# A list scheduler's rules for tiles in advance, changed for the two stages of layer 1's mixer

## The chip, the cores and the metric

The kernel runs on one core of one Trainium2 chip. The metric is the device time of one execution in microseconds (us). Three runs of the kernel before gave a median of 2732.69 us (2731.06 to 2735.65).

## What is computed

A diffusion backbone of two layers over 1024 latent tokens and 256 context tokens, 1024 channels, all in 32-bit floats. Each layer is a mixer and a SwiGLU feed-forward network (FFN), both between RMS norms with learned modulation:

```
for l in range(DEPTH):
    h  = modulate(x, g_pre_mix[l], sh_m, sc_m)
    hc = modulate(ctx, g_pre_mix[l], csh_m, csc_m)
    if l % 2 == 0:
        y, yc = even_mixer(h, hc, ...)
    else:
        y, yc = odd_mixer(h, hc, ...)
    x = x + gt_m * rmsnorm(y, g_post_mix[l])
    h = modulate(x, g_pre_ffn[l], sh_f, sc_f)
    x = x + gt_f * rmsnorm(swiglu(h, w_ffn_in[l], w_ffn_out[l]), g_post_ffn[l])
    ...
return x
```

Layer 0's mixer is dense attention beside a pooling mixer. Layer 1's, the odd one, is attention of 16 heads (4 for keys and values) in a window of 128 tokens on each side plus all context tokens and a sink logit per head. The context stream (`ctx`) is updated in layer 0 only.

## The kernel before, in words

Activations lie transposed: 128 channels on the partitions, tokens along the free axis. The latent tokens are two chunks of 512, L0 and L1; the context is a chunk of 256, CC. Every matmul product is made of three, so that rounded operands give nearly 32-bit results: weights and activations are split in a rounded part (names ending in h: `wh`, `hh`, `th`) and the remainder (`wl`, `hl`, `tl`), and high times high, high times low and low times high are added in one PSUM bank. A weight unit of 128 rows (`wunit`) is loaded into a tile `raw` by a DMA that SP issues; ACT copies it, rounded, to `wh`; DVE (or, for some, POOL) subtracts to get `wl`. A norm is: ACT squares the tile (`S_sq`), DVE adds the squares, PE sums them over partitions with a matrix of ones, ACT takes the root and DVE the reciprocal (`rs`), PE spreads it over the partitions again (`S_rb` against `ident`), and DVE applies it.

`tile_dit` (from L429) doesn't issue instructions. It calls helpers that record operations in a plan, and `Plan.layout` (L241) then writes one order for each engine: it is a list scheduler that always places the operation that can start first by its own estimates of cost and latency. `emit` (L418) issues them in that order, so every profile row carries the line L421. Engines execute their own list in order and meet through semaphores.

Tiles come from three kinds of buffers, which the scheduler assigns too: 38 large ones of 128x1024 (tag Q: `raw`, `wh`, `wl`, `hh`, `yf` and so on), 19 small ones of 128x512 (tag S), and the 8 PSUM banks (tag p). `fits` (L283) refuses an operation that would open a new tile when no buffer is free, when the program in its recorded order would need all of them before that place, and in a third case that the change concerns: `AHEAD_OF` (L32) gives, for each of eight stages, a number `near` and for each kind a number of buffers kept back. An operation whose tile has its first place more than `near` operations past the first one that isn't placed yet may only take a buffer while more than the kept-back number are free.

The stage is the number in `plan.phase` when an operation is recorded. The stages around the change, in the order in which they are recorded:

- stage 7: layer 0's paired FFN, then `ffn_out` (L934) for L0 and CC. Its last group of four weight units gives the products ps_3502 to ps_3512 and ps_3529 to ps_3534 below; `chain` (L626) then applies the norm behind the FFN and the one ahead of the mixer for L0 and CC;
- stage 3: layer 1's projections for L0 and CC (`proj1`, L1462), and attention of L0's first half (`attend1`, L1484), between which `ffn_out` for L1 is spread as filling work (`merge`, L213);
- stage 4: projections for L1, attention of L0's second half and then of L1, with the gate products of the second FFN (`ffn_gates`, L758) as filling work; last `pair_up` (L976), which normalizes L1's result (`postnorm`, L616) and makes from it and L0's the five combinations `th`, `tl` (`prenorm_pair`, L589);
- stages 5 and 6: layer 1's paired FFN (`ffn_pair`, L780) and its output. For every unit `ffn_pair` adds and subtracts raw weights on DVE (`Q_sw`), rounds them on ACT and multiplies them with `th`, `tl`.

Of the kernel before, what the change touches and what calls it, by code (L numbers as in the profile page):

```python
# [28 lines left out]

NQ, NS = 38, 19  # L30
AHEADS = (90, 60, 100, 90, 80)
AHEAD_OF = ((100, {'p': 2, 'Q': 2, 'S': 2}), (250, {'p': 0, 'Q': 10, 'S': 2}), (150, {'p': 2, 'Q': 6, 'S': 0}), (100, {'p': 2, 'Q': 10, 'S': 6}), (250, {'p': 1, 'Q': 4, 'S': 0}), (250, {'p': 1, 'Q': 4, 'S': 2}), (250, {'p': 1, 'Q': 4, 'S': 0}), (250, {'p': 1, 'Q': 4, 'S': 2}))  # L32
MODLATE = (2, 3, 4)
POOLE = 4
OUTM = ("0", "c")
# [35 lines left out]
class Plan:  # L71
# [169 lines left out]
    def layout(self):  # L241
# [41 lines left out]
        def fits(i):  # L283

            for t in ops[i][5]:
                if t not in live:
# [3 lines left out]
                    if a > front and prof[tag][front:a].max() >= self.tag_bufs[tag]:  # L290
                        return tag
                    near, res = AHEAD_OF[ops[i][10]]
                    if a > front + near and len(slots[tag]) <= res.get(tag[0], 0):
# [1360 lines left out]
```

## Time and profile before

| what | value |
|---|---|
| median of three runs | 2732.69 us |
| profiled execution, its own time | 2732.75 us |
| its span in the trace | 2731.0 us |
| granted TensorE clock, mean | 0.982 |
| PE busy | 2617.1 us (96%) |
| DVE busy | 2072.2 us (76%) |
| ACT busy | 1389.4 us (51%) |
| POOL busy | 320.6 us (12%) |

The engines are PE (matrix products), DVE and ACT (elementwise), POOL (elementwise, slower) and SP, which here issues the DMAs. The busy shares are means over stages with different limits; what an order can change is read in the stretch where it changes. Times in the rows are microseconds from the start of the span; "[3.29 <-DVE Q_wl L421]" at the end of a row means that the engine sat idle for 3.29 us until DVE's instruction on Q_wl released it. A granted clock of 1.00 is TensorE's upper level, 2.4 GHz, 0.50 the lower, 1.2 GHz.

### The profile page before, as it was taken

The numbers are of one execution on the slowest core, as the hardware profiler recorded it, in microseconds if no ns is written. First come the engines' busy times: TensorE is split into PE (matmuls) and PEld (weight loads), VectorE is DVE, ScalarE is ACT, GpSimd is POOL, SyncE is SP. The second block draws the span as 40 slices with busy tenths as digits, with TensorE's granted clock in tenths as the row PEclk, the third lists the DMA queues.
The fourth block names the chain that finished last, engine by engine and source line by source line (L and its number), as shares of the span: only waits on it lengthen the run. The fifth ranks groups of instructions, "written<-read, shape, count | busy, mean of one in ns | idle before, by whom it ended". The sixth has DMA issues, their size and how long they took to land.

```text
span 2731.0 us, 39441 instructions
## 1 busy us (share of the span) xinstructions
PE 2617.1 (96%) x13685; PEld 2168.4 (79%) x13685; DVE 2072.2 (76%) x3816; ACT 1389.4 (51%) x2894; POOL 320.6 (12%) x277
## 2 busy tenths in 40 slices
PE   8989898999999999999999998998999999999997
PEld 4766677888888888888877888777878778887887
DVE  5779887866449999875485688898884699896655
ACT  4468875666544333331043467677775544444211
POOL 0354532000020000000011400220000300000001
PEclk9999999999999999999999998999999999999999
DMA  7334467333556666786533634435336547668662
GB/s 286 113 104 144 139 205 281 112 115 118 187 186 213 226 206 231 240 301 242 202 137 112 223 120 166 132 134 157 108 109 216 192 164 252 225 245 332 224 239 78
DMA packets 247176, 506.24 MB, mean 185 GB/s; under 512 B 25280, under 2 KB 86976, under 8 KB 246976
## 3 DMA queue, kind: packets, MB, share of 16 engines
q1 hardware_dynamic: 246976, 503.71, 53.4%
q8 instruction: 108, 1.77, 0.3%
q14 instruction: 92, 0.75, 0.1%
HBM read 363.11 MB, written 136.58 MB: 183 GB/s over the span
## 4 chain that ended last, share of the span: by engine, by line
PE 72%; DVE 10%; ACT 4%; issue 2%; DMA 2%; POOL 1%; SPq 0%; DVEq 0%; ACTq 0%; POOLq 0%
PE ps L421 72%; DVE Q_x L421 1%; DVE S_fw L421 1%; DVE ps L421 1%; DVE mx L421 1%; ACT S_ph L421 1%; ACT Q_p L421 1%; DVE Q_hl L421 1%; DVE Q_yf L421 1%; DVE S_sq L421 1%; DVE Q_tl L421 1%; DVE Q_wl L421 1%; ACT S_p L421 1%; DVE S_pl L421 1%; DVE S_t L421 1%
## 5 line engine op out<-in xcount | busy, mean ns | idle before, releaser
L421 PE MATMUL ps<-Q_ac,Q_wh 128*128 128x512 f32 (+1 forms) x1792 | 492.3, 356 | 0.8 <-ACT Q_wh L421 0.5
L421 PE MATMUL ps<-Q_hh,Q_wh 128*128 128x512 f32 (+1 forms) x992 | 364.6, 377 | 7.0 <-ACT Q_hh L421 3.5
L421 PE MATMUL ps<-Q_hl,Q_wh 128*128 128x512 f32 (+1 forms) x992 | 361.5, 373 | 1.9 <-DVE Q_hl L421 1.7
L421 PEld LDWEIGHTS ps<-Q_ac,Q_wh 128*128 128x128 f32 x1792 | 319.8, 191 | 45.5 <-DVE Q_yf L421 0.6
L421 PE MATMUL ps<-Q_ac,Q_wl 128*128 128x512 f32 (+1 forms) x896 | 317.5, 356 | 6.6 <-DVE Q_wl L421 6.6
L421 ACT ACTIVATE Q_wh<-Q_raw 128x1024 fp32r<-128x1024 f32 (+1 forms) x202 | 203.8, 1028 | 218.3 <-DMA Q_raw<-in_w_ffn_out 105.4
L421 DVE TENSOR_TENSOR Q_wl<-Q_raw,Q_wh 128x1024 fp32r<-128x1024 f32 (+1 forms) x190 | 226.6, 1202 | 95.8 <-ACT Q_wh L421 91.4
L421 PE MATMUL ps<-Q_tl,Q_wh 128*128 128x512 f32 x704 | 276.2, 392 | 2.6 <-DVE Q_tl L421 2.6
L421 PE MATMUL ps<-Q_th,Q_wh 128*128 128x512 f32 x704 | 275.9, 392 | 1.9 <-ACT Q_th L421 1.8
L421 PE MATMUL ps<-Q_kt,S_q 128*128 128x256 f32 (+3 forms) x992 | 254.4, 339 | 17.4 <-DVE Q_x L421 7.2
L421 DVE TENSOR_TENSOR S_pl<-ps,S_ph 128x512 fp32r<-128x512 f32 (+1 forms) x328 | 213.2, 671 | 70.5 <-ACT S_ph L421 65.7
L421 PE MATMUL ps<-Q_hh,Q_wl 128*128 128x512 f32 (+1 forms) x992 | 265.8, 372 | 0.0
L421 DVE TENSOR_TENSOR Q_yf<-Q_yf,ps 128x512 f32<-128x512 f32 (+1 forms) x220 | 130.1, 597 | 164.3 <-PE ps L421 163.8
L421 ACT ACTIVATE S_ph<-ps 128x512 fp32r<-128x512 f32 (+1 forms) x328 | 186.1, 604 | 88.6 <-PE ps L421 86.8
L421 PEld LDWEIGHTS ps<-Q_hh,Q_wh 128*128 128x128 f32 x992 | 189.6, 191 | 39.0 <-ACT Q_hh L421 5.1
L421 PEld LDWEIGHTS ps<-Q_hl,Q_wh 128*128 128x128 f32 x992 | 189.5, 191 | 30.3 <-DVE Q_hl L421 3.6
L421 PEld LDWEIGHTS ps<-Q_kt,S_q 128*128 128x128 f32 x992 | 170.6, 194 | 46.4 <-issue 11.4
L421 PEld LDWEIGHTS ps<-Q_hh,Q_wl 128*128 128x128 f32 x992 | 175.0, 190 | 27.4
L421 PE MATMUL ps<-ident,Q_p 128*128 128x128 f32 x928 | 185.7, 278 | 10.7 <-DVE S_pl L421 3.0
L421 PEld LDWEIGHTS ps<-Q_ac,Q_wl 128*128 128x128 f32 x896 | 171.0, 191 | 29.9 <-DVE Q_wl L421 7.9
L421 ACT ACTIVATE Q_p<-ps,nb 128x256 f32<-128x256 f32 (+1 forms) x336 | 185.5, 562 | 15.1 <-DVE nb L421 14.6
L421 PE MATMUL ps<-Q_th,Q_wl 128*128 128x512 f32 x704 | 188.8, 390 | 0.0
(198 smaller groups left out, 5379.8 us busy)
## 6 DMA issues: line engine op xcount, KB each, us to landing
Q_raw<-in_w_ffn_in SPq DMA_DIRECT2D x132, 512.0 KB, 4.6
mw<-in_w_mod SPq DMA_DIRECT2D x160, 256.0 KB, 3.6
Q_raw<-in_w_ffn_out SPq DMA_DIRECT2D x66, 512.0 KB, 6.3
a_scr_l<-S_act SPq DMA_DIRECT2D x112, 256.0 KB, 2.6
Q_ac<-a_scr_l SPq DMA_DIRECT2D x56, 512.0 KB, 5.9
t_scr<-S_act SPq DMA_DIRECT2D x112, 256.0 KB, 2.2
Q_ac<-t_scr SPq DMA_DIRECT2D x56, 512.0 KB, 5.7
S_q<-q_scr_l SPq DMA_DIRECT2D x192, 128.0 KB, 3.5
```

What stands on the lines that cost most here:

```text
L421: getattr(eng.real, op)(*args, **kw)
```

## The change

One line: two of the eight entries of `AHEAD_OF`, those of stages 3 and 4. Stage 3 may open tiles up to 300 operations ahead freely instead of 100, and past that keeps back 8 large and 3 small buffers instead of 10 and 6. Stage 4 does so for 150 operations instead of 250 and past that keeps back two small buffers where it kept none; its four large ones and the PSUM entries stay.

```diff
-AHEAD_OF = (..., (100, {'p': 2, 'Q': 10, 'S': 6}), (250, {'p': 1, 'Q': 4, 'S': 0}), ...)
+AHEAD_OF = (..., (300, {'p': 2, 'Q': 8, 'S': 3}), (150, {'p': 1, 'Q': 4, 'S': 2}), ...)
```

The instructions stay the same (13,564 matmuls in both); their order and the buffers that tiles get change. As rows of matmuls in a line are counted as one where they repeat, PE's list has 11,742 rows before and 11,746 now; the lists are alike up to row 6,164 and again from about row 10,020 on. Three places, each as a piece of the difference, with - for a row that stood there before and + for one that stands there now.

On DVE, at the end of layer 0's FFN: Q_yf are the FFN's sums, S_sq the squares for the norm behind it, and Q_wl_3519 to Q_wl_3528 the remainders of the last group's four weight units.

```order
 L421 TENSOR_TENSOR Q_yf_2707<-Q_yf_2707,ps_2883 128x256
+L421 TENSOR_TENSOR Q_wl_3519<-Q_raw_3517,Q_wh_3518 128x1024
 L421 TENSOR_TENSOR Q_yf_2711<-Q_yf_2711,ps_2884 128x512
 L421 TENSOR_TENSOR S_sq_3035<-S_sq_3035,S_sq_3041 128x512
```

```order
+L421 TENSOR_TENSOR Q_wl_3522<-Q_raw_3520,Q_wh_3521 128x1024
 L421 TENSOR_TENSOR S_sq_3068<-S_sq_3068 128x256
+L421 TENSOR_TENSOR Q_wl_3525<-Q_raw_3523,Q_wh_3524 128x1024
 L421 RECIPROCAL rs_3043<-rs_3043 128x4
 L421 COPY S_rb_3044<-rs_3043 128x512
+L421 TENSOR_TENSOR Q_wl_3528<-Q_raw_3526,Q_wh_3527 128x1024
 L421 SCALAR_TENSOR_TENSOR Q_yf_2694<-Q_yf_2694,fin,ps_3045 128x512 x2
```

The four remainders stood behind the whole norm of L0's first channels before (Q_wl_3519 behind RECIPROCAL rs_3073, Q_wl_3528 some 30 rows later); now they are made before the first operation that applies that norm. On PE the products ps_3529 to ps_3534 were run with only the first unit's Q_wh first, two matmuls each, and came back for the rest; now each runs its twelve in a row.

On PE, in the last gate products of stage 4 (ps_4946, ps_4947): the sum of squares ps_4930 and the broadcast ps_4933 of the norm in `pair_up`.

```order
 L421 MATMUL ps_4947<-Q_hl_4128,Q_wh_4901 128x512
+L421 MATMUL ps_4930<-ones,S_sq_4922 128x2 x4
 L421 MATMUL ps_4947<-Q_hh_4127,Q_wh_4901 128x512
```

```order
 L421 MATMUL ps_4946<-Q_hl_4132,Q_wh_4898 128x512
+L421 MATMUL ps_4933<-ident,S_rb_4932 128x128 x4
 L421 MATMUL ps_4946<-Q_hh_4131,Q_wh_4898 128x512
```

Counted from the first matmul of ps_4946, the sum stood behind 32 matmuls of 512 columns and stands behind 14; the broadcast behind 61, now 26.

On DVE, at the start of `ffn_pair`: Q_tl_4978 is the last of the combinations, Q_sw the sums of raw weights.

```order
-L421 TENSOR_TENSOR Q_sw_5015<-Q_raw_5013 128x512
-L421 TENSOR_TENSOR Q_sw_5015<-Q_sw_5015,Q_raw_5012 128x512
 L421 RECIPROCAL rs_4943<-rs_4943 128x4
 L421 COPY S_rb_4944<-rs_4943 128x512
```

```order
 L421 SCALAR_TENSOR_TENSOR Q_tl_4978<-Q_x_4921,mod,Q_th_4976 128x512
+L421 TENSOR_TENSOR Q_sw_5015<-Q_raw_5013 128x512
 L421 TENSOR_TENSOR Q_sw_5016<-Q_raw_5012,Q_raw_5013 128x512
+L421 TENSOR_TENSOR Q_sw_5015<-Q_sw_5015,Q_raw_5012 128x512
+L421 TENSOR_TENSOR Q_sw_5035<-Q_raw_5033 128x512
```

The two Q_sw_5015 operations went from ahead of the norm's reciprocal to behind the last combination. On PE the 16 products of Q_wh_5017, made from Q_sw_5015, stood between those of three small weight tiles (S_wh) and now stand behind them.

## Rows read from the trace of the kernel before

**Rows 1.** The page, parts 1 and 4: engines, and the chain that ended last.

```profile
PE 2617.1 (96%) x13685; PEld 2168.4 (79%) x13685; DVE 2072.2 (76%) x3816; ACT 1389.4 (51%) x2894; POOL 320.6 (12%) x277
...
PE 72%; DVE 10%; ACT 4%; issue 2%; DMA 2%; POOL 1%; SPq 0%; DVEq 0%; ACTq 0%; POOLq 0%
```

**Rows 2.** Windows: stretch, length, busy PE, PEld, DVE, ACT, POOL, clock, DMA, GB/s.

```profile
1394.00:1424.00 30.00, 26.26 (x112) 21.63 (x111) 28.39 (x47) 18.71 (x32) 5.58 (x4) 0.89 0.34 123
...
1408.06:1414.89 6.83, 6.76 (x23) 5.88 (x24) 6.12 (x13) 1.45 (x5) 0.73 (x1) 0.50 0.01 4
2175.00:2203.00 28.00, 21.88 (x71) 14.10 (x70) 25.82 (x40) 13.87 (x24) 0.00 (x0) 0.88 0.33 127
1727.00:1822.00 95.00, 89.56 (x513) 74.28 (x512) 85.46 (x239) 75.57 (x207) 23.92 (x20) 0.96 0.45 139
1608.00:1681.00 73.00, 62.39 (x407) 55.38 (x407) 62.24 (x186) 52.76 (x148) 2.43 (x3) 0.88 0.14 44
1460.00:1480.00 20.00, 19.54 (x105) 16.22 (x104) 7.34 (x13) 5.58 (x12) 0.00 (x0) 1.00 0.29 85
```

**Rows 3.** Timeline of PE: the first and the last of 16 matmuls back to back.

```profile
1425.18 0.39 PE L421 MATMUL ps<-Q_hh,Q_wh 128*128 128x512 f32 x1
...
1428.58 0.39 PE L421 MATMUL ps<-Q_hl,Q_wh 128*128 128x512 f32 x1
```

**Rows 4.** Groups of instructions by line and form, PE, 1394 to 1424 us.

```profile
L421 PE MATMUL ps<-Q_ac,Q_wh 128*128 128x512 f32 x63 | 20.5, 417 | 0.5 <-ACT Q_wh L421 0.5
L421 PE MATMUL ps<-Q_ac,Q_wl 128*128 128x512 f32 x27 | 11.6, 428 | 3.3 <-DVE Q_wl L421 3.3
L421 PE MATMUL ps<-ident,S_rb 128*128 128x128 f32 x10 | 2.3, 364 | 0.0
L421 PE MATMUL ps<-ones,S_sq 128*128 128x2 f32 x12 | 2.2, 299 | 0.0
```

**Rows 5.** Timeline around the last group's weights: start, duration, engine, instruction.

```profile
1376.36 10.14 SPq L421 DMA_DIRECT2D Q_raw<-in_w_ffn_out  x4
...
1385.10 0.41 DVE L421 TENSOR_TENSOR Q_yf<-Q_yf,ps 128x256 f32<-128x256 f32 x1
...
1394.90 1.41 DVE L421 SCALAR_TENSOR_TENSOR Q_yf<-Q_yf,fin,ps 128x512 f32<-128x512 f32 x2 [1.88 <-PE ps L421]
...
1401.83 3.01 PE L421 MATMUL ps<-Q_ac,Q_wh 128*128 128x512 f32 x12 [0.45 <-ACT Q_wh L421]
...
1404.38 3.90 ACT L421 ACTIVATE Q_wh<-Q_raw 128x1024 fp32r<-128x1024 f32 x4
...
1406.87 1.20 DVE L421 TENSOR_TENSOR Q_wl<-Q_raw,Q_wh 128x1024 fp32r<-128x1024 f32 x1
...
1408.13 0.79 PE L421 MATMUL ps<-Q_ac,Q_wl 128*128 128x512 f32 x1 [3.29 <-DVE Q_wl L421]
```

**Rows 6.** Waits of PE, 1424 to 1473 us: total, times, longest.

```profile
PE ps L421 <- DVE Q_hl L421: 1.7, 3, 0.9
...
PE ps L421 <- ACT Q_wh L421: 0.5, 1, 0.5
```

**Rows 7.** Timeline around the norm in `pair_up`: DVE, POOL and PE.

```profile
2125.83 0.69 DVE L421 TENSOR_TENSOR S_sq<-S_sq,S_sq 128x512 f32<-128x512 f32 x1 [5.69 <-ACT S_sq L421]
...
2130.03 18.14 POOL L421 TENSOR_TENSOR Q_wl<-Q_raw,Q_wh 128x1024 fp32r<-128x1024 f32 x7 [246.86 <-PE ps L421]
...
2135.76 5.29 DVE L421 TENSOR_TENSOR S_sq<-S_sq,S_sq 128x512 f32<-128x512 f32 x2 [2.79 <-ACT S_sq L421]
...
2141.52 0.95 PE L421 MATMUL ps<-ones,S_sq 128*128 128x2 f32 x8
...
2149.69 0.75 DVE L421 SCALAR_TENSOR_TENSOR Q_y<-Q_y,fin,ps 128x512 f32<-128x512 f32 x1 [6.12 <-PE ps L421]
```

**Rows 8.** Timeline behind the last tl: DVE, then PE.

```profile
2195.13 0.68 DVE L421 TENSOR_TENSOR Q_sw<-Q_raw,Q_raw 128x512 f32<-128x512 f32 x1
...
2199.30 1.07 PE L421 MATMUL ps<-Q_th,Q_wl 128*128 128x512 f32 x4
```

More of the change, by code (lines that the diff above doesn't have):

```diff
@@ L31 @@
 AHEADS = (90, 60, 100, 90, 80)
-AHEAD_OF = ((100, {'p': 2, 'Q': 2, 'S': 2}), (250, {'p': 0, 'Q': 10, 'S': 2}), (150, {'p': 2, 'Q': 6, 'S': 0}), (100, {'p': 2, 'Q': 10, 'S': 6}), (250, {'p': 1, 'Q': 4, 'S': 0}), (250, {'p': 1, 'Q': 4, 'S': 2}), (250, {'p': 1, 'Q': 4, 'S': 0}), (250, {'p': 1, 'Q': 4, 'S': 2}))
+AHEAD_OF = ((100, {'p': 2, 'Q': 2, 'S': 2}), (250, {'p': 0, 'Q': 10, 'S': 2}), (150, {'p': 2, 'Q': 6, 'S': 0}), (300, {'p': 2, 'Q': 8, 'S': 3}), (150, {'p': 1, 'Q': 4, 'S': 2}), (250, {'p': 1, 'Q': 4, 'S': 2}), (250, {'p': 1, 'Q': 4, 'S': 0}), (250, {'p': 1, 'Q': 4, 'S': 2}))
 MODLATE = (2, 3, 4)
```

## The prediction

> **What bounds the kernel now.** I read the page first: PE is busy for 2617.1 of 2731.0 us and holds 72% of the chain that ended last, DVE 10%, ACT 4% [rows 1]. PE takes its instructions in one written order, so a change of order can win only the time in which PE waits or runs at a lower granted clock, in the stretches whose order changes. Against the order before, PE's rows differ from about 1394 us (layer 0's last FFN product, on its way into layer 1) to the first products of layer 1's second FFN stage at about 2200 us; behind that they are alike. So second I read the windows of that part [rows 2], to be read for PE busy, DVE busy and granted clock.
>
> A measure for "lost": back to back, 15 matmuls of 512 columns start within 3.40 us, so one each 0.227 us [rows 3]. From 1394 to 1424 us PE ran 63 + 27 matmuls of 512 columns, 10 of 128x128 and 12 of two columns [rows 4]: 90 x 0.227 + 22 x about 0.1 = 22.6 us, in 30. 7.4 us are lost there. From 2175 to 2203 us it ran 71 matmuls [rows 2], 16.1 us in 28, 11.9 lost. In 1608 to 1681 us PE is busy for 62.39 of 73 us and in 1727 to 1822 for 89.56 of 95 [rows 2].
>
> Third, what PE waits for. At 1401.83 us it starts 12 matmuls that need only the rounded weights Q_wh, and then waits 3.29 us for Q_wl, the remainder that DVE makes [rows 5]. DVE begins it at 1406.87, ACT's Q_wh before it came at 1404.38 for the later three units, while SP had issued those four loads from 1376.36 to 1386.50 [rows 5]. The data were there; the instructions that open new large tiles were not given places. After this wait the granted clock is 0.50 from 1408.06 to 1414.89, the lower of the two levels (1.2 GHz) [rows 2]. In 1424 to 1473 us PE waits 0.5 us for Q_wh and 1.7 for Q_hl, the remainder of the normalized context [rows 6].
>
> **The change, part by part.** Instructions, tiles and arithmetic stay; there is nothing to price but order.
>
> *Stage 3's entry (300, 8, 3 in place of 100, 10, 6).* Q_wl_3519 moves on DVE from behind 1406 us to right behind an addition that ran at 1385.10; the three others move ahead of the first post-norm operation of 1394.90 [rows 5]. The loads of 1376 to 1386 us are in time for that by the timeline, and PE comes to the units at 1401.83 [rows 5], so the four units' products can run straight, in twelves. The 3.29 us wait, its 0.45 us neighbour, and the slow 6.83 us go: the whole 7.4 us. The 0.5 us on Q_wh behind 1424 go too [rows 6]. What is late next is the normalization: the three conversions of some 1.2 us [rows 5] now stand in front of it on DVE, and ACT's ones in front of the inverse root, so its start slips by about 3 us. Against that PE has 42 matmuls instead of 14 ahead of the first sum ps_3054, and 142 instead of 97 ahead of ps_3080: 6.4 and 10.2 us more cover. I leave the 1.7 us on Q_hl where they are. Term: **-7.9 us**; ends 0 (a load lands late and the wait only moves) and -9.6 (these 1.7 go too).
>
> That gain has to pass through the attention. At 1460 to 1480 us DVE is busy for 7.34 of 20 us [rows 2], so nothing of it is backed up there, and from there on all engines begin earlier alike. The 10.6 us of idle PE in 1608 to 1681 stay: the order there hardly changes.
>
> *Stage 4's entry (150 and two small tiles kept, in place of 250 and none).* In the second attention (1727 to 1822 us) pieces of the neighbouring normalization change sides, and score blocks come more singly. DVE is busy there for 85.46 of 95 us [rows 2] and keeps the same instructions between the same attention blocks to within 2 us by the order. PE's idle is 5.4 us, so I take **0**, with -5.4 and, as nothing excludes a loss, +5.4.
>
> At the end of the stage three things move. (a) On PE the sum ps_4930 stands 18 matmuls further forward and the broadcast ps_4933 35, 8.0 us. DVE's post-norm waits 6.12 us for just that broadcast, until 2149.69 [rows 7], so the chain behind it (additions, square sums, th and tl) can begin 8.0 us earlier. (b) Its input, the square sums of 2135.76, took 5.29 us for two operations, where one of the same kind took 0.69 at 2125.83; POOL ran seven Q_wl from 2130.03, waiting for PE until then [rows 7]. In the changed program the first of them writes a tile last read by ps_4869's matmuls, which PE runs some 120 matmuls sooner than those of ps_4896 that it waited for; the last conversion still waits for ps_4896, and ACT's Q_wh for them move forward. POOL's row then ends at about 2130.03 + 18.14 / 7 = 2132.6 and the sums take 1.4 us, in time for PE, which comes to ps_4930 not at 2141.52 [rows 7] but 18 x 0.227 us sooner, at 2137.4. (c) Q_sw_5015 goes from ahead of this chain to behind its last tl, and with it 16 products of Q_wh_5017 that PE now runs while th and tl appear.
>
> The sum of (a) to (c): what follows the last tl on DVE, now at 2195.13 [rows 8], starts 8.0 us sooner, at 2187.1. Three Q_sw operations at about 0.6 us (one is 0.68 and overlaps the next's start a little), 1.0 us for the Q_wh conversion (ACT's four took 3.90 [rows 5]) and 0.2 us that I allow for hand-overs give the first Q_wh_5017 product at 2190.1. Nine matmuls on, the first Q_wl product of this unit starts at 2192.2, against 2199.30 [rows 8]: 7.1 us sooner. But 15 matmuls that lay ahead of it now lie behind, 3.4 us. Term: **-3.7 us**. Ends: -7.1 (the 15 fall into later waits) and +4.3: if the chain begins no sooner, the Q_sw operations make that product 0.9 us later, and 3.4 us are put behind it.
>
> Here a rule has a say. A DVE addition next to POOL's conversions took 2.6 us in place of 0.69 [rows 7]. The Trainium skill's page "SBUF — State Buffer", section "Who interferes with whom", says that a DVE instruction with two SBUF inputs and a GpSimd instruction that reads SBUF exclude each other for a whole instruction. The trace agrees, with 5.29 us for two. By that rule bringing the conversions forward does not remove the collision, it drops it on the additions ahead, as that of 2125.83. As that one has 5.69 us of idle time before it [rows 7], the rule would leave my sum as it is; were POOL to finish only after 2135, the rule would keep the square sums at 5.29 us and take (a)'s gain to about nothing.
>
> **Sum:** -7.9 + 0 - 3.7 = -11.6 us from the profiled execution's own 2732.75 us (span 2731.0 and 1.75 around it), which is within 0.1 us of the runs' median: **2721.2 us**. A measurement of this kernel tells about 0.2% from no change, 5.5 us: faster is under 2727.2, slower over 2738.2.
>
> **Rivals.**
> - *More:* the 1.7 us go too, the FFN start gives 7.1, attention all its 5.4: -22.1, about **2711**. For it: low clock follows waits, so waits that go take their slow matmuls along. Against: DVE has hardly room in 1727 to 1822.
> - *Given back:* the 7.9 us reach 1608 to 1681 us, where PE waits on ACT and DVE, and are waited there; only the FFN start is left: **2729.1**. For: DVE 62.24 of 73 us. Against: those engines' work there hangs on PE's own scores, and moves with it.
> - *Not what it says:* the earlier conversions find their data or buffers late; 0 in place of -7.9, and the FFN start half: **2731**. For: three of the four loads wait for tiles that PE frees only at 1385. Against: 16 us lie between that and PE's need.
> - *Slower:* the start of the second FFN stage. Its place is PE between the last gate product and the first Q_wh_5017 product; with 16 fewer products to run while th and tl are made, and the chain no earlier, it costs the 4.3 us. PE then idles through most of 2176 to 2198, and the 37 matmuls up to the first Q_wl product all run at the lower clock, 0.227 us each more at half the clock, of which about 13 are not hidden in waits: +3. With the first term at 0: 2732.75 + 7.3 = **2740**. What decides is whether DVE's first post-norm operation, now at 2149.69, comes before about 2146. Against: nothing but PE's order holds it today.
>
> **Numbers.** My forecast 52%, more 12%, given back 15%, not what it says 10%, slower 11%. My own case runs from 2714 to 2727. Faster takes nearly all of the first two and a third of the middle two's spread: 0.70. Same: 0.20. Slower: 0.10. The range of 2712 to 2731 us leaves out most of the slower case and the lower half of "more", 2 in 10.
>
> **What would show it.** In the changed profile: no wait for Q_wl over 1 us and no clock of 0.50 before the attention at 1450; the context's products ending some 8 us sooner; then equal shifts through 2130. POOL's seven conversions beginning some 25 us sooner in the program's course; the square sums back at 0.7 us; post-norm 8 us sooner still, and one wait for Q_wh at the start of the second FFN stage. I am wrong if the shift at 1600 us is not seen any more at 1700, or if the second attention's PE idle moves by more than 4 us either way.

## The result, and the profile after

The changed kernel takes 2718.68 us in the median of four runs (2714.70 to 2720.03), against 2734.17 us (2731.06 to 2735.80) before on the same chip: 0.9944 of the time, 95% interval 0.9932 to 0.9957, so 15 us faster. Run again later as `changed_again`, it gave 0.9937 (0.9926 to 0.9949). The profiled execution takes 2714.70 us (span 2712.9), against 2732.75. The forecast was 2721.2 us in a range of 2712 to 2731, faster with 0.70.

The page of the changed kernel, parts 1 and 4, which answer to [rows 1]: the engines' work is unchanged, and the span is 18 us shorter.

```profile
PE 2612.4 (96%) x13685; PEld 2167.9 (80%) x13685; DVE 2071.1 (76%) x3816; ACT 1385.3 (51%) x2894; POOL 318.8 (12%) x277
...
PE 73%; DVE 9%; ACT 4%; issue 2%; DMA 2%; POOL 1%; SPq 0%; DVEq 0%; ACTq 0%; POOLq 0%
```

Its windows. All but the second answer to one of [rows 2], and each is placed earlier by about the lead that the kernel has by then (13, 13, 15, 15 to 18 and 20 us):

```profile
1381.00:1411.00 30.00, 29.65 (x151) 24.88 (x150) 25.39 (x41) 18.08 (x29) 4.87 (x3) 1.00 0.56 192
1411.00:1460.00 49.00, 48.48 (x260) 41.28 (x259) 45.54 (x84) 24.02 (x46) 8.65 (x7) 1.00 0.44 131
1593.00:1666.00 73.00, 62.77 (x404) 55.60 (x403) 61.41 (x184) 52.40 (x154) 2.42 (x3) 0.91 0.14 44
1712.00:1804.00 92.00, 89.70 (x525) 74.58 (x524) 82.35 (x232) 73.13 (x200) 23.79 (x20) 1.00 0.42 131
2155.00:2183.00 28.00, 23.37 (x89) 17.85 (x88) 25.36 (x39) 15.00 (x24) 0.00 (x0) 0.88 0.45 160
```

PE is busy for 29.65 of 30 us in the first, where [rows 2] had 26.26, at a clock of 1.00 in place of 0.89: it does 151 matmuls in place of 112. The second holds 260 matmuls, and 49 us at that place in the kernel before (1424 to 1473) held 234. In the first attention (third line) PE idles for 10.2 us where it idled for 10.6, in the second (fourth) for 2.3 in place of 5.4.

For a table of places I took the moment at which PE starts the first matmul into a PSUM tile, in every trace that the study has, and the time between two such moments: A from ps_3506 to ps_3130 (end of layer 0's FFN, start of the projections; 1393 to 1470 us before), B on to ps_3435 (projections and first attention), C on to ps_4896 (second attention with its projections, and the gate products), D on to ps_5154 (norm in `pair_up`, start of the second FFN stage). Traces in which PE's order at a place is that of before are averaged apart from those in which it is that of the change (and nothing else was edited there); orders that are neither are left out.

| place | before | after | old order, mean (traces) | new order, mean (traces) | new less old |
|---|---|---|---|---|---|
| A | 76.5 | 64.0 | 77.8 (4) | 65.6 (7) | -12.2 |
| B | 164.3 | 166.7 | 165.4 (4) | 166.9 (9) | +1.5 |
| C | 494.4 | 489.5 | 493.0 (3) | 488.8 (6) | -4.2 |
| D | 128.5 | 125.3 | 128.2 (6) | 124.9 (5) | -3.3 |

The sum is -18.2 us, within the timed intervals of both runs (0.9944 and 0.9937 make -15 and -17 us). Stretches whose order is the same differ from trace to trace by 2 to 4 us (C's old order 490.7 to 494.4, D's 126.5 to 129.6), so B's figure is hardly outside the scatter, and no single pair of traces settles a term of 3 us; means of several do it better.

In C the scatter has a visible source, the granted clock. With the old order, `before` has two stretches of 3.41 us at 0.50 in its second attention (from 1732.33 and 1817.66 us), `stage3_kept_only` two like them (from 1728.04 and 1813.37), and `only_pair_up`, with the same order of PE, has neither; its C is 3.7 and 3.2 us shorter than theirs. The windows of the two stretches in `before`, then of the 513 matmuls in `only_pair_up` that take 95 us in [rows 2]:

```profile
1732.33:1735.74 3.41, 3.41 (x9) 2.63 (x9) 2.23 (x12) 2.64 (x10) 0.00 (x0) 0.50 0.89 268
1817.66:1821.07 3.41, 3.37 (x10) 2.67 (x10) 3.41 (x7) 2.62 (x8) 0.43 (x1) 0.50 0.96 323
```

```profile
1727.70:1819.00 91.30, 86.48 (x513) 72.04 (x512) 84.63 (x239) 75.01 (x205) 22.52 (x18) 1.00 0.47 142
```

At 0.50 matmuls of 512 columns start 0.43 us apart (1411.60, 1412.02, 1412.45 in the kernel before) in place of 0.227, so 6.8 us of it cost an estimated 3. No trace with the new order has such a stretch there. Against `only_pair_up` alone the new order is 1.9 us shorter: the rest of C's difference goes with the clock, which differs between executions of one order. A's longest trace with the new order, `stage3_entry_only` with 67.6 us, has 3.41 us at 0.50 too (from 1443.46).

### The profile page after: what moved, and what is told of

Read it like the earlier page. It is cut to its first block, busy times and chain, and to the rows that moved or that the text cites. A ratio compares the mean times of both kernels' runs of the same rounds, so it can differ in the third digit from the quotient of the medians.

```text
span 2712.9 us, 39459 instructions
## 1 busy us (share of the span) xinstructions
PE 2612.4 (96%) x13685; PEld 2167.9 (80%) x13685; DVE 2071.1 (76%) x3816; ACT 1385.3 (51%) x2894; POOL 318.8 (12%) x277
## 4 chain that ended last, share of the span: by engine, by line
PE 73%; DVE 9%; ACT 4%; issue 2%; DMA 2%; POOL 1%; SPq 0%; DVEq 0%; ACTq 0%; POOLq 0%
PE ps L421 73%; DVE S_fw L421 1%; DVE Q_x L421 1%; DVE ps L421 1%; DVE mx L421 1%; ACT S_ph L421 1%; ACT Q_p L421 1%; ACT Q_wh L421 1%; DVE Q_hl L421 1%; DVE Q_tl L421 1%; DVE Q_wl L421 1%; DVE S_pl L421 1%; DVE Q_yf L421 0%; ACT S_p L421 0%; DVE S_t L421 0%
## 5 line engine op out<-in xcount | busy, mean ns | idle before, releaser
L421 PE MATMUL ps<-ident,Q_p 128*128 128x128 f32 x928 | 185.2, 277 | 10.2 <-DVE S_pl L421 3.1
```

Source lines behind the costliest of these rows:

```text
L421: getattr(eng.real, op)(*args, **kw)
```

## Experiments

Four theories stood against each other: the time comes from the end of the FFN alone; from three places; the start of the second FFN stage matters more, or less, than forecast; and only one of the numbers in the table acts.

**Each place by itself.** `splice` calls `layout` with two tables and joins two orders at a matmul: all up to it comes from HEAD, the rest from TAIL.

```diff
-        for i in self.layout():
+        for i in self.splice():
...
+HEAD = ((300, {'p': 2, 'Q': 8, 'S': 3}), (150, {'p': 1, 'Q': 4, 'S': 2}))
+TAIL = ((100, {'p': 2, 'Q': 10, 'S': 6}), (250, {'p': 1, 'Q': 4, 'S': 0}))
+CUT = 8440
```

That is `only_ffn_end`. `only_second_attention` has the old entry of stage 3 and the new one of stage 4 in HEAD, the old ones in TAIL and the cut at 10700; `only_pair_up` has the old entries in HEAD, the new ones in TAIL and the cut at 10700.

> The changed order up to matmul 8440 of 13564 (the end of layer 0's FFN and the first attention), then the order before. Theory 'three places that add up': the end of layer 0's FFN gives about 11 us in the trace and the first attention takes about 2 of them back, so some 9 us less than the kernel before, 2723 to 2727. Rival 'given back': the attention behind it waits the gain away, within 3 us of the kernel before. Rival 'only together': the later stretches need the earlier start, so this part alone gives under half of 9.

> The order before, but the changed order from the projections of stage 4 to the end of the second attention (nothing ahead of it, nothing of pair_up). Theory 'three places': -5 to -7 us, the place that the prediction took at 0. Rival, the prediction's own 0: within 2 us of the kernel before, and what the trace shows there is the clock's or an earlier start's doing.

> The order before up to matmul 10700, then the changed order (pair_up and the start of the second FFN stage alone). Theory: -4 us, from the norm chain that begins 8 us sooner against 3.4 us of products put behind; 2729 to 2731. Rival: the products put behind cost as much as the chain gives, within 1 us of before. In the trace POOL's first conversion should start some 25 us sooner and the two square sums take 0.7 us each.

| kernel | median us (runs) | ratio, 95% interval | A, C, D us |
|---|---|---|---|
| only_ffn_end | 2725.22 (5) | 0.9967, 0.9954 to 0.9980 | 65.0, 493.6, 128.8 |
| only_second_attention | 2729.10 (11) | 0.9983, 0.9975 to 0.9992 | 77.8, 489.7, 127.1 |
| only_pair_up | 2726.76 (11) | 0.9983, 0.9973 to 0.9992 | 78.6, 490.7, 125.1 |

Three places act, not one. The ratios make -9.0, -4.6 and -4.6 us, together -18, so they add up. C of `only_pair_up` is low although its order is old there; that is the clock told of above, and the timed ratios, from many executions, are the better evidence. PE's waits from its second attention's projections on, in the kernel before (1681 to 1775 us), then in the changed one (1670.4 to 1758.5):

```profile
PE ps L421 <- DMA Q_kt<-S_kk: 2.0, 1, 2.0
PE ps L421 <- DVE S_pl L421: 0.5, 1, 0.5
PE ps L421 <- ACT S_p L421: 0.2, 1, 0.2
```

```profile
PE ps L421 <- ACT Q_mh L421: 0.8, 1, 0.8
PE ps L421 <- DVE Q_ml L421: 0.3, 1, 0.3
PE ps L421 <- DVE S_pl L421: 0.2, 1, 0.2
```

The 2.0 us in which PE waited for keys on their way through a DMA (Q_kt) are gone. SP's row for those eight transfers (ns for one shortest, median and longest; first to last issue), before, then after:

```profile
L421 SPq DMA_DIRECT2D Q_kt<-S_kk x8: 461/568/596, 1727.1 to 1733.0; - x8
```

```profile
L421 SPq DMA_DIRECT2D Q_kt<-S_kk x8: 503/574/1236, 1714.2 to 1719.3; - x8
```

The products of the keys that were already there start at 1726.92 us before and at 1717.45 after: the issue came 0.2 us behind that start and now comes 3.2 us ahead of it. But the 2.0 us are not all gain: from ps_3688 to ps_3809, which spans this place, the mean goes from 72.8 us (71.2 to 73.6 in three traces) to 71.8. The 71.2 is `only_pair_up`'s, which waits 1.4 us for the same keys but has no clock of 0.50 behind it; the other two wait 2.0 and 1.9 us and have one. What the place gives beyond that is not traced to a single wait.

**Which number acts.** The kernels below have the table of before but for the entry shown.

```
stage 3's entry
before:               (100, {'p': 2, 'Q': 10, 'S': 6})
stage3_entry_only:    (300, {'p': 2, 'Q': 8, 'S': 3})
stage3_kept_only:     (100, {'p': 2, 'Q': 8, 'S': 3})
stage3_distance_only: (300, {'p': 2, 'Q': 10, 'S': 6})

stage 4's entry
before:               (250, {'p': 1, 'Q': 4, 'S': 0})
stage4_entry_only:    (150, {'p': 1, 'Q': 4, 'S': 0})
```

> Only stage 3's entry changed (300, 8, 3), stage 4's as before: the end of layer 0's FFN is as in the changed kernel, the second attention has an order of its own, pair_up is as before. Theory 'three places': -9 us or a little more, never the whole -15; 2721 to 2727. Rival 'stage 3's entry does it all': -14 or more.

> Of stage 3's entry only the kept-back buffers (8 large and 3 small in place of 10 and 6), still 100 instructions ahead; stage 4 as before. Theory 'the distance of 300 does it': the 3 us wait for Q_wl_3519 and the lower clock behind it stay, 0 to -2 us against before. Rival 'the kept-back buffers do it': -7 or more, like stage 3's whole entry.

> Of stage 4's entry only the distance (150 in place of 250), stage 3 as before; its order is the same as with the two small tiles kept back too. Theory: the sum of its two places, second attention -2 to -4.6 and start of the second FFN stage -4 to -4.6: -6 to -9 us against before, 2723 to 2727. Rival: the two don't add up, -4.6 or less in size.

> Of stage 3's entry only the distance (300 in place of 100), 10 large and 6 small buffers kept back as before; stage 4 as before. Theory: nearly the order of stage 3's whole entry, so its time within 2 us, 2721 to 2726. Rival, from the run with the kept-back buffers alone (-5 us): the two add up, and the distance alone gives only some 7 us, 2726 to 2729.

| kernel | median us (runs) | ratio, 95% interval | A, C, D us |
|---|---|---|---|
| stage3_entry_only | 2723.06 (6) | 0.9955, 0.9941 to 0.9969 | 67.6, 490.9, 128.5 |
| stage3_kept_only | 2728.52 (12) | 0.9981, 0.9971 to 0.9992 | 72.3, 493.9, 126.5 |
| stage3_distance_only | 2720.69 (5) | 0.9956, 0.9944 to 0.9968 | 64.0, 491.7, 129.6 |
| stage4_entry_only | 2726.32 (11) | 0.9967, 0.9954 to 0.9980 | 78.3, 490.0, 124.7 |

The distance of 300 does all that stage 3's entry does (0.9956 against 0.9955); the smaller reserve alone takes 5 us, more than the one theory and less than the other had for it, and adds nothing to the distance. With the smaller reserve alone PE still waits for Q_wl, and only that and a Q_wh are left of the waits of 1390 to 1470 us:

```profile
PE ps L421 <- DVE Q_wl L421: 3.9, 1, 3.9
PE ps L421 <- ACT Q_wh L421: 0.5, 1, 0.5
```

Stage 4 acts by the 150: with the two small buffers kept back or not, the lists of all engines are the same but for two neighbouring instructions of ACT (S_sq_4121 and Q_wh_4086) that change places. The two entries alone make -12.3 and -9.0 us, 4 to 6 more together than the whole change. That would fit an overlap in C, where stage 3's entry alone also changes the order, but it is not shown: by the timed runs 4 to 6 us is about the uncertainty of such a sum, and that kernel's 490.9 us in C are no shorter than `only_pair_up`'s 490.7 with the old order.

**The four conversions back behind the norm** (`late_conv`: the changed order, but DVE's four Q_wl stand in one block behind RECIPROCAL rs_3073, the place that Q_wl_3519 had before).

```diff
+LATE = "Q_wl3417_3519", "Q_wl3420_3522", "Q_wl3423_3525", "Q_wl3426_3528"
+BEFORE = "ps3427_3529"
...
+        queue["DVE"] = dve[:k] + mine + dve[k:]
```

> The changed order whole, but DVE's four conversions Q_wl_3519 to Q_wl_3528 put back behind the norm (right ahead of the first sum that needs their products); PE's and ACT's lists as changed. Theory: the early conversions are what the 12 us at the end of layer 0's FFN hang on; PE then waits at its first unit from about 1402 us on, longer than in the kernel before since it can't run the other rows first and since the third unit's load waits for the first conversion's tile: 8 to 13 us over the changed kernel's 2719, 2727 to 2732. Rival: the norm, no longer behind the conversions, comes 3 us sooner and PE's longer list covers the rest, under 4 us over the changed kernel.

It took 2725.20 us (6 runs), 0.9966 (0.9955 to 0.9978), 8 us more by the ratios than `changed_again` beside it (3 to 13 by the two intervals). A is 76.2 us. PE's waits from 1390 to 1465 us:

```profile
PE ps L421 <- DVE Q_wl L421: 7.3, 1, 7.3
PE ps L421 <- ACT Q_hh L421: 2.5, 1, 2.5
PE ps L421 <- DVE Q_hl L421: 0.6, 1, 0.6
```

DVE's order of these four instructions is worth 8 of the 9 to 12 us of A, on the timed runs, with PE's twelves as they are: PE's grouping alone does not make the gain, DVE's early remainders are needed. What they give with PE's old grouping was not run.

**The norm in `pair_up`** (`late_sum`: the changed order, with the two sums and two broadcasts put back on PE where they stood).

```diff
+FIRST = ('ps4828_4930', 'ps4831_4933', 'ps4840_4942', 'ps4843_4945')
```

> The changed order whole, but with the four sums and broadcasts of pair_up (ps_4930, ps_4933, ps_4942, ps_4945) put back on PE where they stood; POOL's early conversions and the Q_sw operations behind the last tl stay. Theory of the prediction: the norm chain begins 8 us later again while the 16 products stay behind, so the start of the second FFN stage costs about 8 us more than in the changed kernel and about 4 more than before: 2725 to 2729, PE waiting longer there. Rival 'POOL': the gain at this place came from POOL's conversions out of the way of the square sums, not from PE's order; then within 2 us of the changed kernel's 2719.

It took 2729.71 us (12 runs), 0.9990 (0.9978 to 1.0003): 13 us more than the changed kernel by the ratios (0.9990 less 0.9944), where the prediction's (a) had 8. D is 141.2 us. The timeline of PE, its two longest waits:

```profile
2141.11 0.80 PE L421 MATMUL ps<-Q_hh,Q_wh 128*128 128x512 f32 x1 [5.67 <-ACT S_gs L421]
...
2161.74 0.54 PE L421 MATMUL ps<-Q_hh,Q_wh 128*128 128x512 f32 x1 [3.55 <-ACT S_gs L421]
```

These waits exist in neither kernel. ACT's list still has the root and the squares ahead of the copies S_gs that free PE's banks, so PE, with the sum and the broadcast put late, waits for copies that wait for its own sum and broadcast. D also holds 23.9 us at a clock of 0.50 there, 6.8 in the changed kernel. The run shows that PE's place for the sum and ACT's list belong together; it doesn't price the sum's place by itself, and what that alone is worth in time stays open.

It does settle what the norm chain starts by. POOL's conversions are as early as in the changed kernel and the square sums take 1.42 us, yet DVE's first post-norm operation comes 20.9 us behind PE's first matmul into ps_4896 (2111.99), as before (2149.69 and 2128.83, also 20.9) and not 12.9 as in the changed kernel (2126.21 and 2113.30). DVE's timeline of `late_sum`:

```profile
2118.92 1.42 DVE L421 TENSOR_TENSOR S_sq<-S_sq,S_sq 128x512 f32<-128x512 f32 x2 [2.79 <-ACT S_sq L421]
...
2132.92 1.40 DVE L421 SCALAR_TENSOR_TENSOR Q_y<-Q_y,fin,ps 128x512 f32<-128x512 f32 x2 [6.32 <-PE ps L421]
```

So the 8.0 us of (a) are PE's place for the sum and the broadcast, and the rival 'POOL' is out for them.

**Q_sw first** (`sw_first`, and `sw_first_again`: the changed order, with the two Q_sw_5015 operations and the 16 products of Q_wh_5017 put back ahead of the norm).

```diff
+FIRST = ('Q_sw4913_5015', 'Q_wh4915_5017')
```

> The changed order whole, but Q_sw_5015's two operations, the conversion to Q_wh_5017 and its 16 products back where the order before had them, between the sum of squares and the th and tl. Theory: the 15 products that were put behind cost 3.4 us in the changed kernel, and the first Q_wl product can come up to 1 us sooner; so 3 to 4.5 us under the changed kernel's 2719, 2714 to 2716. Rival: DVE ends the production of tl later by the two operations (1.2 us) and ACT by the conversion (1.0 us), and the gain is under 1.5 us.

> The kernel with Q_sw_5015 and its 16 products ahead once more, on one chip with the changed kernel. Theory from its first trace: the start of the second FFN stage gains 1.6 us and a wait for Q_wl some 40 us later takes 1.8 back, so the same as the changed kernel within 1.5 us. Rival: 3 us under it.

> The changed kernel once more, as a measure for the run with Q_sw ahead: -14 to -16 us against before, 2717 to 2720.

2717.46 us, 0.9935 (0.9920 to 0.9950), and 2715.21, 0.9938 (0.9926 to 0.9950), against 0.9937 (0.9926 to 0.9949; 2715.94 us) for the changed kernel beside the second. No difference: the products do fill PE (8.51 of 10 us busy from 2163.3 to 2173.3 us, where the changed kernel, 3.3 us earlier there, has 5.44), and PE then waits further on. PE's waits of `sw_first`, 2150 to 2240 us:

```profile
PE ps L421 <- DVE Q_wl L421: 1.7, 2, 1.6
PE ps L421 <- ACT Q_wh L421: 1.7, 1, 1.7
PE ps L421 <- DVE Q_tl L421: 1.3, 2, 0.8
PE ps L421 <- ACT Q_th L421: 0.2, 1, 0.2
```

The theory of 3 to 4.5 us is out. What bounds the start of that stage instead is likely DVE, which does the same work in either order; it is read from its busy time, and no kernel with less of that work was run. In the changed kernel it is busy for all of these 10 us:

```profile
2160.00:2170.00 10.00, 5.44 (x21) 3.60 (x20) 10.00 (x17) 6.18 (x11) 0.00 (x0) 0.90 0.41 143
```

No kernel of the study is measurably faster than the changed one.

## Why the prediction was right, and where it was wrong

**End of layer 0's FFN: forecast -7.9, measured about -12 (-9 by the timed kernel with that place alone).** The mechanism is as told: the remainders come early, the wait and the slow stretch behind it go. The timeline of DVE in the changed kernel answers to [rows 5]:

```profile
1385.20 1.22 DVE L421 TENSOR_TENSOR Q_wl<-Q_raw,Q_wh 128x1024 fp32r<-128x1024 f32 x1 [0.18 <-PE ps L421]
...
1391.05 1.22 DVE L421 TENSOR_TENSOR Q_wl<-Q_raw,Q_wh 128x1024 fp32r<-128x1024 f32 x1
1392.65 1.23 DVE L421 TENSOR_TENSOR Q_wl<-Q_raw,Q_wh 128x1024 fp32r<-128x1024 f32 x1
...
1396.14 1.23 DVE L421 TENSOR_TENSOR Q_wl<-Q_raw,Q_wh 128x1024 fp32r<-128x1024 f32 x1 [0.79 <-ACT Q_wh L421]
```

Four remainders by 1397.4 us, where the first began at 1406.87; no wait for Q_wl and, in this trace, no clock of 0.50 is left. The step that failed is "I leave the 1.7 us on Q_hl where they are". Its own working spoke against it: the sums had 6.4 and 10.2 us more cover and the norm slipped by only 3. Of PE's waits from 1381 to 1460 us two are left, where the kernel before had 6.7 us from 1394 to 1473 (3.6 for Q_wl, 1.7 for Q_hl, 0.9 for Q_wh, 0.5 for Q_hh):

```profile
PE ps L421 <- DVE Q_hl L421: 0.5, 1, 0.5
PE ps L421 <- DVE S_rb L421: 0.3, 1, 0.3
```

And those waits had cost more than their listed idle time. The timeline of PE in the kernel before, in that part:

```profile
1441.09 0.39 PE L421 MATMUL ps<-Q_hl,Q_wh 128*128 128x256 f32 x1
1442.03 0.39 PE L421 MATMUL ps<-Q_hh,Q_wh 128*128 128x256 f32 x1 [0.55 <-ACT Q_hh L421]
1442.90 0.39 PE L421 MATMUL ps<-Q_hl,Q_wh 128*128 128x256 f32 x1 [0.49 <-DVE Q_hl L421]
1443.12 0.28 PE L421 MATMUL ps<-Q_hh,Q_wh 128*128 128x256 f32 x1
1444.32 0.39 PE L421 MATMUL ps<-Q_hl,Q_wh 128*128 128x256 f32 x1 [0.92 <-DVE Q_hl L421]
```

Four matmuls start within 3.23 us, with 1.96 us listed as waiting; starts of such matmuls without a wait lie 0.17 to 0.23 us apart there, so 2.3 to 2.5 us are lost. I measured the first 30 us by the pitch of matmuls and the next 49 by the list of waits. By the pitch (0.227 us for 512 columns, 0.12 for 256, about 0.1 for the small ones) the 345 matmuls of the whole 79 us need 66.3 us before, and the 408 that now fit in need 77.0: 12.7 us were lost and 2.0 are. Of the 12.7, 6.7 are listed waits, and an estimated 3 are the 6.83 us at a clock of 0.50.

**Attention: forecast no loss; B shows +1.5, about the scatter.** All but that of the lead passes through. The rival in which it is given back there is out.

**Second attention: forecast 0 (±5.4), measured about -4.** The failed step is "keeps the same instructions between the same attention blocks": I compared DVE's list, and took the stretch from 1727 us, while what moved starts ahead of it, in the projections: the keys' two last operations and their transfers, whose issue by SP comes 3.4 us earlier against PE. The clock of 1712 to 1804 us is 1.00 where that of [rows 2] was 0.96, two stretches of 0.50 for which the forecast has no term; with the same order `only_pair_up` has none of them and is 3.7 us shorter in C. What the timed runs show is the gain (-4.6 us alone, -2.2 to -6.8); how much of it is the clock and which wait holds most of it stays open.

**Start of the second FFN stage: forecast -3.7, measured -3.3 (timed alone -4.6).** (b) came as told: POOL's last Q_wl ends at 2116.9, and the square sums that took 5.29 us in [rows 7] take 1.42. (a) too: the first post-norm operation starts at 2126.21, 23.5 us earlier than in [rows 7], where the lead by ps_4896 is 15.5 (2113.30 against 2128.83 us): the 8.0 us of the forecast, and `late_sum` shows them to be PE's place for the sum. DVE's timeline:

```profile
2114.79 2.65 DVE L421 TENSOR_TENSOR S_sq<-S_sq,S_sq 128x512 f32<-128x512 f32 x1 [2.86 <-ACT S_sq L421]
2120.23 1.42 DVE L421 TENSOR_TENSOR S_sq<-S_sq,S_sq 128x512 f32<-128x512 f32 x2 [2.79 <-ACT S_sq L421]
2126.21 1.41 DVE L421 SCALAR_TENSOR_TENSOR Q_y<-Q_y,fin,ps 128x512 f32<-128x512 f32 x2 [1.71 <-PE ps L421]
```

(c) was wrong in kind: not one wait for Q_wh, but PE stands before th and a small weight, since the 16 products that could have filled that time are put behind. PE's waits from 2150 to 2240 us:

```profile
PE ps L421 <- ACT Q_th L421: 3.6, 1, 3.6
PE ps L421 <- ACT S_wh L421: 1.0, 1, 1.0
```

The first Q_wl product comes at 2176.28, 23.0 us earlier than in [rows 8], so 7.5 beyond the lead where the forecast had 7.1. By the end of D some 4 of these are gone, about the 3.4 that I took off for the 15 products put behind. But `sw_first` puts these products ahead again and wins nothing, so they are not what took them: that the term came out at the right size is luck. The step that failed is to charge PE for work put behind, where PE's own work was not the bound; DVE's likely is.

**The collision of DVE and POOL** moved as the forecast worked it out from the Trainium skill's rule (page "SBUF — State Buffer", section "Who interferes with whom"): the addition at 2114.79 takes 2.65 us beside POOL's conversion of 2114.50, and has 2.86 us of idle time before it. Trace and rule agree. It costs nothing here: DVE waits another 2.79 us for ACT behind it.

**Rivals.** "More" was nearest in mechanism (waits take their slow matmuls along), 2711 us against 2718.68 measured. "Not what it says" and "slower" are out: the data were in time, and DVE's post-norm came at 2126.21 us, 2141.7 with the lead of 15.5 added, ahead of the 2146 that was to decide.

## What to carry to other kernels

Price what a removed wait gives back over the whole stretch behind it by PE's back-to-back pitch, not by the listed idle time, which here was about half. In a scheduled order, look for loads that have landed while the first instruction on them stands behind a chain it doesn't need: that instruction's place on its engine was worth 8 us here, and a longer distance for opening tiles moved it. Before a term of 2 to 4 us is read from two traces, see how far the same stretch scatters where nothing was changed, and compare the granted clock of the two: in C 3.7 of the 4.9 us between the two kernels' traces go with it.

## What was not expected of the hardware

Starts behind a short wait cost more than the wait listed: 1.20 us from start to start where 0.92 were listed, and 0.87 where 0.49 were, in place of 0.17 to 0.23 without a wait. DVE's additions that start while POOL converts are slow: 2.54, 2.02, 2.58 and 2.65 us for the four single additions between 2101 and 2117 us of the changed kernel, 0.71 each for the two right behind them. Additions of DVE that start 0.16 us ahead of one of POOL's (2127.53 and 2129.45) take 0.69. And the lower clock is not a fixed part of an order: `only_pair_up` goes through the second attention without it, where `before` has it twice with the same order of PE.
